# Transposes in front of the attention layer: from TensorE to transposing transfers, with the last products with V in another PSUM bank

## The chip, the cores and the metric

One Trainium2 chip, one core. The time is device microseconds for one execution, the median of the runs shown.

## What is computed

A two-layer decoder trunk on 256 tokens of width 1024, all in float32. The first layer mixes tokens with a gated recurrence, the second with attention whose logits carry a forget-gate bias; every layer has a SwiGLU half-step before and behind the mixer, and every part is wrapped in RMS norms. The part around the change, cut from the reference:

```python
f = swiglu(rms_norm(h, ffn1_pre_g), w_gate, w_up, w_down)
h = h + 0.5 * rms_norm(f, ffn1_post_g)
hn = rms_norm(h, mix_pre_g)
q = (hn @ w_q) * HEAD_DIM ** -0.5
logits = q @ k.T + c[q_rows] - c[k_rows]        # causal, 16 heads of 64
o = softmax(logits) @ v
h = h + rms_norm(o @ w_o, mix_post_g)
```

## The kernel before, in words

**Tiles.** The 256 tokens are two halves, t = 0 and t = 1, of 128 rows each; h0 and h1 hold them, 128 x 1024. TensorE is fed in a split form: a float32 operand is cut into a high and a low part (whi and wlo for weights, xhi and xlo for the stream), and a product is three matmuls, high by high, high by low, low by high. Weights come in pieces of 512 KB into five "raw" buffers (SP's queue issues the loads); ScalarE makes whi (L173) and VectorE wlo (L177), which also frees the raw buffer. Items with a load and a split are prepared ahead; a "slot" (t, i) is the work of item i for half t.

**From h to x.** A product needs x = h scaled by a gain, transposed: eight "k tiles" of 128 x 128. `enter` runs when a sub-layer's sums pf are done: sums of squares on ScalarE, the factor rstd on GpSimd, `t1 = pf * gain` and `h = t1 * rstd + h` on VectorE (L298, L311). Some ticks later `inputs` transposes h. There are two ways:

- On TensorE: `to_tp` (L226), four transposes per 512 columns into a PSUM bank; then VectorE multiplies by the gain (L234), ScalarE writes xhi (L235), VectorE writes xlo (L240).
- By a transposing transfer, for 512 columns: `planes` (L212, GpSimd) sorts the upper and lower 16 bits of each number into two planes, `swap` (L216) issues a DMA that transposes 16-bit elements, `join` (L220, GpSimd) puts the numbers together again; then the gain on VectorE and xhi on ScalarE (`turned_to_x`, L258 and L259), and xlo (L240).

Before the change the end of the half-step in front of attention uses TensorE for all eight k tiles of both halves.

**Queues.** TensorE's order is written out by hand: the stage around attention is the string ATT_ORDER, in which a digit is a slot of that half, l, n, t and v are logits, normalisation, transposes of the probabilities and products with V, each followed by the half. It begins `0 0 0 0 0 0 0 l0 0 1 n0 l0 1 1 t0 n0 1 l0 v0 1 t0 n0 l0 1`: eight slots of q for half 0 and then those of half 1, with the first half's softmax between them. `defer(n, fn)` calls fn n + 1 slots later. On VectorE, ScalarE, GpSimd and SP a scheduler decides the order at build time, and at run time each engine works through its queue strictly in that order.

**Attention.** `heads_T` scales the queries (L1044) and transposes them, on TensorE for half 0 (L1057), by a transfer for half 1. `logits` writes into two "gt" banks (L1194); VectorE adds the bias and takes the extreme (L1203), corrects it (L1207, L1208); ScalarE takes exponentials (L1210); VectorE normalises (L1216, L1217). `turn` transposes the result (L1223) and `values` multiplies with V into one of four "mm" banks, "po" (L1237). The bias of half 1 is a table of 2 MB in DRAM, fetched by GpSimd's queue at the start of the stage (`att_rows`, L1038).

**PSUM.** "mm" has four banks (sums of products), "gt" two (logits, transposes of h), "tr" two.

Of the kernel before, what the change touches and what calls it, by code (L numbers as in the profile page):

```python
# [17 lines left out]
P = 128  # L18
# [25 lines left out]
def trunk_kernel(ctx: ExitStack, tc: tile.TileContext, A: dict, out: bass.AP):  # L44
    nc = tc.nc
# [5 lines left out]
    hpool = ctx.enter_context(tc.tile_pool(name="h", bufs=1))  # L51
# [29 lines left out]
    def defer(n, fn):  # L81
        pend.append([n, fn])
# [23 lines left out]
    h = [hpool.tile([P, D], F32, tag=f"h{t}", name=f"h{t}") for t in range(2)]  # L106
# [23 lines left out]
    gT = cpool.tile([P, 56], F32, name="gT")  # L130
# [79 lines left out]
    def planes(dst, src):  # L210

        nc.gpsimd.tensor_copy(dst.rearrange("p (h f) -> p h f", h=2), src.bitcast(U16).rearrange("p (f h) -> p h f", h=2))  # L212

    def swap(turned, halves):

        tc.keep_in_program_order(nc.sync.dma_start(turned.rearrange("p (a b) -> p a b", b=P), halves, transpose=True))  # L216

    def join(dst, turned):

        nc.gpsimd.tensor_copy(dst, turned.rearrange("p (h f) -> p h f", h=2))  # L220
# [17 lines left out]
    def x_lower(xg, dest, n):  # L238
        gi, xh, xl = dest
        nc.vector.tensor_tensor(xl[:, 4 * n:4 * n + 4, :], xg, xh[:, 4 * n:4 * n + 4, :].bitcast(F32), ALU.subtract)  # L240
# [5 lines left out]
            for n, v in enumerate(xg):  # L246
                x_lower(v, dest, n)

    def turned_to_x(v, dests, more):

        with tc.high_priority():
            xs = []
            for i, (gi, xh, xl) in enumerate(dests):
                xg = v if i == len(dests) - 1 else more()
                g = gT[:, gi + 4:gi + 8].unsqueeze(2).to_broadcast([P, 4, P])
                xs.append(xg.rearrange("p (a b) -> p a b", a=4))
                tc.keep_in_program_order(
                    nc.vector.tensor_tensor(xs[i], v.rearrange("p (a b) -> p a b", a=4), g, ALU.mult))  # L258
                tc.keep_in_program_order(nc.scalar.activation(xh[:, 4:, :], xs[i], AF.Copy))  # L259
            for xg, dest in zip(xs, dests):  # L260
                x_lower(xg, dest, 1)

    def to_x_tiles(tps, dest):

# [15 lines left out]
    def stat(t):  # L280
        ss = new_ss()
        square_sum(h[t], ss[:, 0:1])
        rs[t] = rstd_of(ss, 1)

    def enter(t, dests, pf, gb, half, last=False, normed=False, wait=3, spare=None):
# [3 lines left out]
        t1 = []  # L289
# [26 lines left out]
        if last:  # L316
            return

        by_transfer = (spare or t == 1) and not (half and (len(dests) == 1 or t == 0)) and not normed
        if by_transfer:  # L320
            a = spare() if t == 0 else hpool.tile([P, 512], F32, tag="t1", name=nm("hp"), bufs=2)
            with tc.high_priority():
# [2 lines left out]
        def inputs():  # L325
            tps = [to_tp(h[t], n) for n in range(1 if by_transfer else 2)]
            for dest in dests:
                to_x(tps, dest)
            stat(t)
            if by_transfer:  # L330
                b = spare() if t == 0 else spool.tile([P, 512], F32, tag="junk", name=nm("ht"), bufs=1)
                with tc.high_priority():
                    swap(b.bitcast(U16), a.bitcast(U16))
                defer(0, lambda: join(a.bitcast(U16).rearrange("p (f h) -> p h f", h=2), b.bitcast(U16)))
                defer(1 + 2 * t, lambda: turned_to_x(a, dests, spare))

        def norm():
            with tc.high_priority():
# [22 lines left out]
        if normed:  # L361
            norm()
            settled[0] = True
        else:
            defer(wait, inputs)

    def gain_bcast(src):
        gb = hpool.tile([P, D], F32, tag="gb", name=nm("gb"), bufs=1)
# [239 lines left out]
    pools = {}  # L608
# [426 lines left out]
    def att_rows():  # L1035

        tc.keep_in_program_order(nc.scalar.activation(warm, mhalf, AF.Exp))
        tc.keep_in_program_order(nc.gpsimd.dma_start(att["bias1"], kv["bias1"]))  # L1038

    def heads_T(ps, t, n, scale, dst):  # L1040

# [130 lines left out]
    def attention(t):  # L1172
# [54 lines left out]
        def values(hg):  # L1227

            hds = range(hg * per, (hg + 1) * per)
            if hds[0] % 8 == 0:  # L1230
                box["po"] = mmbank()
            po, pT = box["po"].rearrange("p (a b) -> p a b", a=4), box["pT", hg]
            for j in range(0, per, 2):
                for k in range(nk):
                    for s in range(2):
                        hd = hds[j + s]
                        nc.tensor.matmul(po[s * HD:(s + 1) * HD, hd % 8 // 2, :], kv["v"][k][:, hd * HD:(hd + 1) * HD],  # L1237
                                         pT[:, (j + s) * nk + k, :], start=k == 0, stop=k == nk - 1)
# [266 lines left out]
```

## Time and profile before

| | us |
|---|---|
| median of 3 runs | 964.48 (964.27 to 964.72) |
| the profiled execution | 965.18 |
| its span in the trace | 963.5 |
| TensorE busy | 954.8 (99%) |
| VectorE, ScalarE, GpSimd busy | 646.0, 527.5, 236.5 |
| TensorE's granted clock | 0.999 |

The stage of the change lies between 700 and 770 us of the span: the half-step's last products end at 709, the queries' products run from 709 to 740, the softmax from 721 on, and w_o's products from 741 to 779. "Busy" of TensorE is modelled from the matmuls' sizes; waits are better seen in the distance between starts.

### The profile page before, as it was taken

The numbers are of one execution on the slowest core, as the hardware profiler recorded it, in microseconds if no ns is written. First come the engines' busy times: TensorE is split into PE (matmuls) and PEld (weight loads), VectorE is DVE, ScalarE is ACT, GpSimd is POOL, SyncE is SP. The second block draws the span as 40 slices with busy tenths as digits, with TensorE's granted clock in tenths as the row PEclk, the third lists the DMA queues.
The fourth block names the chain that finished last, engine by engine and source line by source line (L and its number), as shares of the span: only waits on it lengthen the run. The fifth ranks groups of instructions, "written<-read, shape, count | busy, mean of one in ns | idle before, by whom it ended". The sixth has DMA issues, their size and how long they took to land.

```text
span 963.5 us, 12847 instructions
## 1 busy us (share of the span) xinstructions
PE 954.8 (99%) x4559; PEld 789.6 (82%) x4559; DVE 646.0 (67%) x845; ACT 527.5 (55%) x750; POOL 236.5 (25%) x229
## 2 busy tenths in 40 slices
PE   9999999999999999999999999999999999999997
PEld 6888888898878888888898888888887788888885
DVE  6758774578997756664686566665488876666642
ACT  7446454568986555444565445444366865444431
POOL 2812230130003323230023623224022133232200
PEclk9999999999999999999999999999999999999999
DMA  8788996485338687676559979879763478777731
GB/s 283 227 229 252 250 291 196 143 222 166 128 110 244 203 238 215 201 245 193 138 158 313 249 223 262 223 190 289 227 255 102 121 210 260 208 225 234 217 110 44
DMA packets 153158, 199.84 MB, mean 207 GB/s; under 512 B 71390, under 2 KB 90182, under 8 KB 152966
## 3 DMA queue, kind: packets, MB, share of 16 engines
q1 hardware_dynamic: 150406, 192.11, 67.4%
q0 software_dynamic: 2080, 6.38, 2.3%
q8 instruction: 36, 0.59, 0.2%
q10 hardware_dynamic: 608, 0.53, 0.2%
q14 instruction: 28, 0.23, 0.1%
HBM read 182.19 MB, written 3.16 MB: 192 GB/s over the span
## 4 chain that ended last, share of the span: by engine, by line
PE 95%; DVE 2%; ACT 1%; issue 1%; POOL 0%; DMA 0%; POOLq 0%; DVEq 0%; ACTq 0%
PE mm L454 16%; PE mm L455 16%; PE mm L458 16%; PE mm L183 13%; PE mm L185 13%; PE mm L184 13%; PE gt L824 2%; PE mm L1340 1%; PE mm L190 1%; PE mm L191 1%; PE mm L192 1%; ACT pe L1210 1%; PE gt L226 1%; PE tr L127 0%; DVE wlo L177 0%
## 5 line engine op out<-in xcount | busy, mean ns | idle before, releaser
L177 DVE TENSOR_TENSOR wlo<-raw,whi 128x1024 fp32r<-128x1024 f32 (+5 forms) x329 | 423.0, 1293 | 213.9 <-ACT whi L173 212.4
L173 ACT ACTIVATE whi<-raw 128x1024 fp32r<-128x1024 f32 (+5 forms) x329 | 341.6, 1045 | 295.8 <-PE mm L458 107.2
L454 PE MATMUL mm<-whi,xhi 128*128 128x512 f32 x656 | 256.7, 391 | 0.0
L455 PE MATMUL mm<-wlo,xhi 128*128 128x512 f32 x656 | 255.5, 389 | 0.0
L458 PE MATMUL mm<-whi,xlo 128*128 128x512 f32 x656 | 202.2, 389 | 0.0
L454 PEld LDWEIGHTS mm<-whi,xhi 128*128 128x128 f32 x656 | 123.2, 188 | 25.9 <-issue 0.7
L458 PEld LDWEIGHTS mm<-whi,xlo 128*128 128x128 f32 x656 | 123.1, 188 | 26.0 <-DVE xlo L240 0.2
L455 PEld LDWEIGHTS mm<-wlo,xhi 128*128 128x128 f32 x656 | 123.2, 188 | 25.3 <-DVE wlo L177 0.3
L183 PE MATMUL mm<-whi,hhi 128*128 128x512 f32 x352 | 137.2, 390 | 0.0
L185 PE MATMUL mm<-whi,hlo 128*128 128x512 f32 x352 | 137.0, 389 | 0.0
L184 PE MATMUL mm<-wlo,hhi 128*128 128x512 f32 x352 | 137.0, 389 | 0.0
L569 POOL COPY pl<-prod 128x1024 uint16<-128x1024 uint16 (+1 forms) x48 | 67.7, 1410 | 168.9 <-DMA prod<-pl 168.9
L556 POOL COPY pl<-prod 128x1024 uint16<-128x1024 uint16 (+1 forms) x48 | 70.1, 1460 | 141.8 <-DVE prod L553 74.4
L185 PEld LDWEIGHTS mm<-whi,hlo 128*128 128x128 f32 x352 | 66.1, 188 | 13.7
L183 PEld LDWEIGHTS mm<-whi,hhi 128*128 128x128 f32 x352 | 66.1, 188 | 13.7
L184 PEld LDWEIGHTS mm<-wlo,hhi 128*128 128x128 f32 x352 | 66.1, 188 | 13.6
L198 POOL TENSOR_SCALAR nv<-ss 128x1 f32<-128x1 f32 x22 | 11.4, 517 | 252.8 <-ACT junk L205 252.8
L553 DVE SCALAR_TENSOR_TENSOR prod<-mm,rstd,sil 128x512 f32<-128x512 f32 (+1 forms) x48 | 33.7, 703 | 29.1 <-PE mm L458 24.8
L544 ACT ACTIVATE sil<-mm,rstd 128x512 f32<-128x512 f32 (+1 forms) x48 | 31.1, 650 | 32.4 <-PE mm L458 24.8
L575 DVE TENSOR_TENSOR hlo<-pl,hhi 128x512 fp32r<-128x512 f32 (+1 forms) x48 | 41.2, 858 | 3.6 <-ACT hhi L574 3.6
L183 PE MATMUL mm<-whi,xhi 128*128 128x512 f32 (+1 forms) x112 | 42.8, 382 | 0.0
L185 PE MATMUL mm<-whi,xlo 128*128 128x512 f32 (+1 forms) x112 | 42.5, 379 | 0.0
(235 smaller groups left out, 1067.8 us busy)
## 6 DMA issues: line engine op xcount, KB each, us to landing
raw<-in_ffn_w_down_dram SPq DMA_DIRECT2D x88, 512.0 KB
raw<-in_ffn_w_up_dram SPq DMA_DIRECT2D x80, 512.0 KB
raw<-in_ffn_w_gate_dram SPq DMA_DIRECT2D x78, 512.0 KB
raw<-in_rg_w_in_dram SPq DMA_DIRECT2D x10, 504.0 KB
raw<-in_rg_w_out_dram SPq DMA_DIRECT2D x10, 504.0 KB
raw<-in_ffn_w_gate_dram SPq DMA_DIRECT2D x19, 256.0 KB
raw<-in_ffn_w_up_dram SPq DMA_DIRECT2D x16, 256.0 KB
raw<-in_rg_w_in_dram SPq DMA_DIRECT2D x8, 512.0 KB
```

The costliest lines, as they stand in the source:

```text
L173: up = nc.scalar.activation(hi[:parts, c:c + m], rawv[:, c:c + m], AF.Copy)
L177: nc.vector.tensor_tensor(lo[:parts, c:c + m], rawv[:, c:c + m], hi[:parts, c:c + m].bitcast(F32), ALU.subtract)
L183: nc.tensor.matmul(ps, xh, wh, start=first, stop=False)
L184: nc.tensor.matmul(ps, xh, wl, start=False, stop=False)
L185: nc.tensor.matmul(ps, xl, wh, start=False, stop=last)
L454: nc.tensor.matmul(ps, get_x(t, k)[0], u.hi[:, c], start=k == 0, stop=False)
L455: nc.tensor.matmul(ps, get_x(t, k)[0], u.lo[:, c], start=False, stop=False)
L458: nc.tensor.matmul(ps, get_x(t, k)[1], u.hi[:, c], start=False, stop=k == nk - 1)
L553: nc.vector.scalar_tensor_tensor(pr[:, :nn], ps, rs[t][:, 0:1], s, ALU.mult, ALU.mult)
L556: nc.gpsimd.tensor_copy(halves.rearrange("p (h f) -> p h f", h=2), pr[:, :nn].bitcast(U16).rearrange("p (f h) -> p h f", h=2))
L569: nc.gpsimd.tensor_copy(halves.rearrange("p (f h) -> p h f", h=2), turned.rearrange("p (h a) b -> p h (a b)", h=2))
L575: keep(nc.vector.tensor_tensor(lv, x, hv.bitcast(F32), ALU.subtract))
```

## The change

At the end of the half-step in front of attention, half 0 now takes only its k tiles 0 to 3 through TensorE and 4 to 7 through one transposing transfer. Half 1 takes all eight through two transfers (`whole_inputs`), with planes made in `enter` itself. The fetch of the bias table is deferred by seven slots more. The products with V of the second eight heads of half 1 are summed in a "gt" bank in place of an "mm" bank.

```diff
-    def turned_to_x(v, dests, more):
+    def turned_to_x(v, dests, more, n=1):
...
-        by_transfer = (spare or t == 1) and not (half and (len(dests) == 1 or t == 0)) and not normed
+        by_transfer = (spare or t == 1) and not (half and len(dests) == 1 + (t == 0)) and not normed
+        whole = half and len(dests) == 1 and t == 1 and not normed
+        if whole:
+            with tc.high_priority():
+                hp = [hpool.tile([P, 512], F32, tag="t1", name=nm("hp"), bufs=2) for _ in range(2)]
+                for n in range(2):
+                    planes(hp[n].bitcast(U16), h[t][:, n * 512:(n + 1) * 512])
...
+        def whole_inputs():
+            ht = [pools["a"].tile([P, 512], F32, tag="pT", name=nm("ht"), bufs=4).bitcast(U16) for _ in range(2)]
+            with tc.high_priority():
+                for n in range(2):
+                    swap(ht[n], hp[n].bitcast(U16))
+            stat(t)
+            with tc.high_priority():
+                for n in range(2):
+                    join(hp[n].bitcast(U16).rearrange("p (f h) -> p h f", h=2), ht[n])
+            for n in range(2):
+                defer(3, lambda n=n: turned_to_x(hp[n], dests, None, n))
...
-            defer(wait, inputs)
+            defer(wait, whole_inputs if whole else inputs)
...
-        tc.keep_in_program_order(nc.gpsimd.dma_start(att["bias1"], kv["bias1"]))
+        defer(7, lambda: tc.keep_in_program_order(nc.gpsimd.dma_start(att["bias1"], kv["bias1"])))
...
-                box["po"] = mmbank()
+                box["po"] = mmbank() if t == 0 or hds[0] == 0 else gtbank()
```

`turned_to_x` with n = 0 writes k tiles 0 to 3, with n = 1 tiles 4 to 7. Line numbers behind `turned_to_x` rise by 18 in the changed kernel at most (L1203 becomes L1221).

Where this moves instructions, the built programs show. First VectorE, from the end of the half-step for half 1 to the first reductions of logits; before (h_75 is h1, xg the product of gain and turned h, htok the scaled queries, gt the logits, ISA the reduction):

```order
L177 TENSOR_TENSOR wlo_6338<-raw_6335,whi_6337 128x1024
L234 TENSOR_TENSOR xg_6383<-gt_6373,gT 128x512
L234 TENSOR_TENSOR xg_6386<-gt_6378,gT 128x512
L1044 TENSOR_SCALAR htok_6404<-mm_6354,rstd_6270 128x512
L240 TENSOR_TENSOR xlo<-xg_6383,xhi 128x4x128
L240 TENSOR_TENSOR xlo<-xg_6386,xhi 128x4x128
L1203 ISA pe_6443,mx_6442<-gt_6431,bias_2952 128x128
```

and the same place in the changed kernel (hp is h in planes and then turned):

```order
L177 TENSOR_TENSOR wlo_6341<-raw_6338,whi_6340 128x1024
L1062 TENSOR_SCALAR htok_6394<-mm_6356,rstd_6263 128x512
L258 TENSOR_TENSOR hp_6334<-hp_6334,gT 128x512
L240 TENSOR_TENSOR xlo<-hp_6334,xhi 128x4x128
L258 TENSOR_TENSOR hp_6335<-hp_6335,gT 128x512
L1221 ISA pe_6439,mx_6438<-gt_6427,bias_2952 128x128
L1221 ISA mx_6438 128x1
L240 TENSOR_TENSOR xlo<-hp_6335,xhi 128x4x128
L1221 ISA pe_6439,mx_6438<-gt_6428,bias_2952 128x128
```

Both multiplications by the gain, and with them the two joins, now stand ahead of the first reduction of the first half's logits, and the last low part behind the first reduction. Next GpSimd in the changed kernel, from the write of h1 on (before, the table's fetch, `L1038 DMA`, stood ahead of the first of these nv rows, and no hp row was there):

```order
L212 COPY hp_6334<-h_75 128x1024
L212 COPY hp_6335<-h_75 128x1024
L198 TENSOR_SCALAR nv_6382<-ss_6379 128x1
L200 TENSOR_TENSOR rstd_6384<-nv_6382,mhalf 128x1
L220 COPY hp_6334<-ht_6375 128x2x512
L220 COPY hp_6335<-ht_6376 128x2x512
L1056 DMA bias_6350<-bias1d 128x4096
L212 COPY pl_6535<-htok_6533 128x1024
```

Two planes, two joins and the fetch now stand in one row ahead of the second half's queries (pl and htok). And SP's queue in the changed kernel, from the last loads of w_q on:

```order
L161 DMA raw_6295<-in_attn_w_q_dram 128x2x512
L216 DMA_TRANSPOSE hp_6265<-hp_6217 128x8x128
L161 DMA raw_6301<-in_attn_w_q_dram 128x2x512
L164 DMA raw_6338<-in_attn_w_o_dram 128x1024
L164 DMA raw_6478<-in_attn_w_o_dram 128x1024
L164 DMA raw_6500<-in_attn_w_o_dram 128x1024
L164 DMA raw_6512<-in_attn_w_o_dram 128x1024
L387 DMA gb_6498<-in_mix_post_g_dram 128x1024
L216 DMA_TRANSPOSE ht_6375<-hp_6334 128x8x128
L216 DMA_TRANSPOSE ht_6376<-hp_6335 128x8x128
```

The three transposing transfers are new there: the first half's ahead of the last load of w_q, the second half's behind the gain row gb and ahead of w_o's fifth piece; the other rows keep their order. On VectorE the first half's multiplication stands between the splits of the sixth and seventh w_q pieces, and its low part between the two t1 rows of half 1. TensorE's order loses the three blocks of four transposes and is otherwise unchanged.

More of the change, by code (lines that the diff above doesn't have):

```diff
@@ L254, in turned_to_x @@
                 xg = v if i == len(dests) - 1 else more()
-                g = gT[:, gi + 4:gi + 8].unsqueeze(2).to_broadcast([P, 4, P])
+                g = gT[:, gi + 4 * n:gi + 4 * n + 4].unsqueeze(2).to_broadcast([P, 4, P])
                 xs.append(xg.rearrange("p (a b) -> p a b", a=4))
@@ L258, in turned_to_x @@
                     nc.vector.tensor_tensor(xs[i], v.rearrange("p (a b) -> p a b", a=4), g, ALU.mult))
-                tc.keep_in_program_order(nc.scalar.activation(xh[:, 4:, :], xs[i], AF.Copy))
+                tc.keep_in_program_order(nc.scalar.activation(xh[:, 4 * n:4 * n + 4, :], xs[i], AF.Copy))
             for xg, dest in zip(xs, dests):
-                x_lower(xg, dest, 1)
+                x_lower(xg, dest, n)
     def to_x_tiles(tps, dest):
```

## Prediction

> **What bounds the kernel now.** I read first the busy shares of the page and the chain that ended last, then TensorE's own waits, and then one stage, 700 to 770 us, row by row on each engine.
>
> ```profile
> PE 954.8 (99%) x4559; PEld 789.6 (82%) x4559; DVE 646.0 (67%) x845; ACT 527.5 (55%) x750; POOL 236.5 (25%) x229
> PE 95%; DVE 2%; ACT 1%; issue 1%; POOL 0%; DMA 0%; POOLq 0%; DVEq 0%; ACTq 0%
> PE gt L1194 <- POOL qT L220: 0.2, 1, 0.2
> ```
>
> TensorE is busy 99% and is 95% of the chain. TensorE's own list of waits has next to nothing in this stage; the one that matters is the last row. So an instruction taken off TensorE is time won, and a wait added on TensorE is time lost, since nothing behind has slack to win it back. The chain of waits inside this window leaves TensorE and comes back to it there:
>
> ```profile
> 722.54 0.47 PE mm L458 x2
> 723.03 0.75 DVE htok L1044
> 724.19 2.12 ACT pe L1210 x11
> ...
> 728.55 0.91 DVE wlo L177
> 729.70 0.76 DVE htok L1044
> 730.57 1.91 POOL pl L212
> 732.50 3.07 DMA htok<-pl
> 735.62 1.69 POOL qT L220
> 737.35 1.14 PE gt L1194 x8
> ```
>
> From the first half's softmax (exponentials on ScalarE from 724 on) through the second half's queries to the logits at 737.35 no link is idle. Whatever delays the softmax beyond its present place delays the logits by as much.
>
> **The change part by part: TensorE's instructions that go.** The timeline of TensorE, start and length:
>
> ```profile
> 702.69 0.39 PE L185 MATMUL mm<-whi,hlo 128*128 128x512 f32 x1
> 702.92 1.04 PE L226 MATMUL gt<-ident,h 128*128 128x128 f32 x8
> ...
> 704.02 0.39 PE L184 MATMUL mm<-wlo,hhi 128*128 128x512 f32 x1
> ...
> 771.06 0.60 PE L226 MATMUL gt<-ident,h 128*128 128x128 f32 x4
> ...
> 771.73 0.39 PE L184 MATMUL mm<-wlo,oh 128*128 128x512 f32 x1
> ```
>
> A matmul follows the next after 0.23 us (702.69 to 702.92). A block of eight costs 704.02 - 702.92 - 0.23 = 0.87 us, a block of four 771.73 - 771.06 - 0.23 = 0.44 us. The first half goes from eight to four, -0.43; the second from eight to none, -0.87. Sum **-1.30 us**.
>
> **The bank.** At the second half's first product with w_o:
>
> ```profile
> 763.60 0.40 PE L185 MATMUL mm<-whi,ol 128*128 128x512 f32 x1
> 764.08 0.50 PE L183 MATMUL mm<-whi,oh 128*128 128x512 f32 x1
> 764.41 0.39 PE L184 MATMUL mm<-wlo,oh 128*128 128x512 f32 x1
> ```
>
> Two steps take 0.81 where two free ones take 0.46: the second accumulator waits for a bank. With one tile more outside the four "mm" banks this wait has no cause, **-0.35 us**; at worst it stays, 0. The product moved into the logits' bank must now wait until VectorE has read the last logits there. It is the third product with V behind those logits, with two slots of w_o between, so I put it at 0; if VectorE falls behind TensorE there, the wait shows at that product.
>
> **What is added.** Each transfer is a copy on GpSimd (planes), a transposing transfer on SP's queue, a copy back on GpSimd (join), a multiplication on VectorE, and the two parts on ScalarE and VectorE. Rows for the same work elsewhere, and for the write of h0:
>
> ```profile
> 742.11 1.24 SPq L216 DMA_TRANSPOSE htok<-pl  x1
> ...
> 741.04 1.04 POOL L212 COPY pl<-htok 128x1024 uint16<-128x1024 uint16 x1 [3.74 <-DVE mx L1208]
> 745.27 1.37 POOL L220 COPY qT<-htok 128x1024 uint16<-128x1024 uint16 x1 [3.19 <-DMA htok<-pl]
> ...
> 766.42 1.90 POOL L212 COPY qT<-h 128x1024 uint16<-128x1024 uint16 x1 [1.58 <-DVE h L311]
> ...
> 700.89 1.42 DVE L311 SCALAR_TENSOR_TENSOR h<-t,rstd,h 128x512 f32<-128x512 f32 x2 [0.38 <-POOL rstd L200]
> ```
>
> A transfer is 3.1 us from issue to the copy it releases (742.11 to 745.27). A planes copy is 1.04 to 1.9 us; right behind the write of h, where VectorE goes on with weights, it is 1.90, and that case is ours. Joins run 1.37 to 1.7; I take 1.5.
>
> First half: h0 is written by 702.3 on VectorE (last row). Planes to 704.2, landed 707.3, join to 708.8, multiplication to 709.5, ScalarE's part to 710.3, VectorE's low part to about 711.9. TensorE, 0.43 earlier, wants the first at 711.55 (the slot at 711.98 today) and the second 0.9 later, at 712.45. Hidden, with 0.5 us left. It has a price all the same, for VectorE's order is fixed. Today:
>
> ```profile
> 708.03 2.35 DVE L177 TENSOR_TENSOR wlo<-raw,whi 128x1024 fp32r<-128x1024 f32 x2
> 710.30 1.28 DVE L298 TENSOR_TENSOR t<-mm,gb 128x512 f32<-128x512 f32 x2
> 711.51 1.41 DVE L311 SCALAR_TENSOR_TENSOR h<-t,rstd,h 128x512 f32<-128x512 f32 x2
> ```
>
> Between the two weight parts now stands the multiplication, which waits for the join until 708.8, and between the two t rows the low part. The write of h1 starts at about 712.5 and not at 711.51: 1.0 late, although TensorE ends earlier. SP's transfer stands ahead of the last load of w_q, which leaves some 2 us later for it; its use near 720 is far off, so that is free.
>
> Second half: the first half of h1 is there at 713.2. Planes to 715.1 and 717.0, landed 718.2 and 720.1, joins to 719.7 and 721.6, second multiplication about 721.7 to **722.3**. TensorE wants this x at 721.5 for tiles 0 to 3 (ready about 721.1) and at 724.6 for 4 to 7 (ready 723): hidden again. But VectorE's fixed order has the logits of the first half behind that multiplication. Today they start when TensorE delivers them:
>
> ```profile
> 721.44 0.29 DVE L1203 CUSTOM_DVE_ANT_0 pe<-gt,bias 128x128 f32<-128x128 f32 x1 [3.19 <-PE gt L1194]
> 723.70 0.15 DVE L1208 TENSOR_TENSOR mx<-mx,cq 128x4 f32<-128x4 f32 x1
> 725.78 0.69 DVE L1217 TENSOR_TENSOR pe<-pe,sm 128x512 f32<-128x512 f32 x1
> 727.40 0.60 PE L1223 MATMUL tr<-ident,pe 128*128 128x128 f32 x4
> ```
>
> TensorE would deliver at 720.1, and the 3.19 us of idle time in that row is the whole cover; the chain needs until 722.3. Behind the first reduction the last low part waits for ScalarE until 723.0 and ends at 723.6; three reductions (0.63), the queries' scaling (0.7) and the maximum (0.3) end at 725.3, where L1208 ends today at 723.8. So the softmax comes **1.5 us later than today**, where TensorE is 1.3 us earlier. The transposes at 727.40 have 0.9 us of slack today (pe is ready at 726.47): they wait until 728.0. The chain quoted above then carries the full 1.5 us to the logits at 737.35, which wait today already. The gain of 1.30 is thus consumed and 1.5 us added: TensorE waits some 2.8 us in all in two or three places (the transposes at 727.40 or the turned queries just ahead of them, and the logits at 737.35).
>
> The table bias1 is now fetched behind the joins:
>
> ```profile
> 711.49 0.63 POOL L1038 DMA_DIRECT2D bias<-bias1d  x1
> bias<-bias1d POOLq DMA_DIRECT2D x1, 2048.0 KB, 11.8
> 738.51 0.42 DVE L1203 CUSTOM_DVE_ANT_0 pe<-gt,bias 128x256 f32<-128x256 f32 x1 [0.41 <-PE gt L1194]
> ```
>
> Issued at 722 with 11.8 us it lands at 734, ahead of its use at 738.5 or later: 0. It leaves the queues free for the transposing transfers, which is in the 3.1.
>
> **Sum**: the stage ends at +1.5, the bank gives back 0.35, so **+1.15 us**. On the profiled execution (965.18, span 963.5) that is 966.33; on the median shown, 964.48, which lies 0.7 lower, it is **965.6**.
>
> Bounds. Everything hidden: -1.30 - 0.35 = -1.65. Copies as short as recorded (1.04 and 1.37): h1 0.9 earlier, planes done 2.6 earlier in all, and the multiplication, behind the low part of tiles 0 to 3, at 720.3: 2.0 less, net -0.85. On the other side a pair of transfers seen behind weight loads:
>
> ```profile
> 535.78 1.24 SPq L216 DMA_TRANSPOSE ktok<-pl  x1
> 537.76 1.43 SPq L216 DMA_TRANSPOSE ktok<-pl  x1
> ...
> 539.91 2.17 POOL L1072 COPY kT<-ktok 128x1024 uint16<-128x1024 uint16 x1 [2.18 <-DMA ktok<-pl]
> 542.52 2.29 POOL L1072 COPY kT<-ktok 128x1024 uint16<-128x1024 uint16 x1 [0.43 <-DMA ktok<-pl]
> ```
>
> 4.1 and 4.8 us to the copies, which themselves took 2.2: the same here adds 1.0 to 1.7 us to the +1.15, up to +2.9. I take 3.1, since the ring is nearer to that of 742.11: ahead of our transfers stand one load of w_o and the gain row, 2 us and more earlier.
>
> [...] The trace has the one at 742.11 moving at some 210 GB/s:
>
> ```profile
> GB/s 0 0 0 0 0 0 0 0 0 0 0 0 10 133 218 218 215 228 205 218 202 212 205 184 213 134 28 0 0 0 0 0 0 0 0 0 0 0 0 0
> ```
>
> **Rivals.** (1) The cover is long enough: copies find VectorE idle, the second multiplication ends by about 719.5 to 720.3, TensorE hardly waits, and the time is 962.8 to 963.6. For it: the 3.19 us of idle time on VectorE, and copies of 1.04. Against: it needs 2 us or more from a chain of seven links, and the copies right behind h in the rows are the long ones. (2) Slower: the two transfers of the second half come late, behind loads in SP's ring or because the first half's transfer moved h1. Place: the second join. Price: 1 us for each us, from the +1.15; it passes 0.2% (1.93 us, about what a measurement of this kernel can tell from no change) when the join ends 0.8 us later than 721.6. At the precedent's lengths: 966.6 to 967.4. If the first half's transfer takes 4.8 us too, TensorE waits at 712 as well and it is 969. (3) bias1 takes over 16 us, and the reductions at 738.5 wait: each us one us, 966 to 968; against it, w_o is loaded by then and little else wants the queues.
>
> **How the numbers follow.** My case (net -0.8 to +1.9) 0.62; rival 1, 0.11; rival 2, 0.22; rival 3, 0.05. No reckoned case gains over 1.93 us; I leave 0.04 of rival 1 for what I can't see. Faster 0.04, same 0.62 + 0.07 = 0.69, slower 0.27. The range, 963.0 to 967.4, takes in the short copies and the pair's lengths, and leaves out the fully hidden case and the slowest.
>
> **What would show it.** In the changed kernel's timeline: TensorE's blocks at 702.9 (four) and 713 (none); the second multiplication of hp ending near 722.3 and VectorE's first reduction right behind it; TensorE waiting near 726 to 728 for pe and before the second half's first logits, now near 738.9; no wait at the second half's second w_o accumulator. I am wrong if the first reduction starts by 720.8 (then a gain), or if the joins start after 719 and 721 (then rival 2).

## The result and the profile after

The changed kernel takes 967.74 us (median of 7 runs, 967.50 to 968.34), the kernel before 964.56 in the runs beside it: ratio 1.0032, 95% interval 1.0023 to 1.0042. That is 3.2 us slower, where the prediction had 1.15 and 967.4 as its upper end. The profiled execution took 967.74, its span is 966.0.

The profiled executions of the kernels here stand up to 2.6 us apart before the stage of the change begins (the write of h0 starts between 700.02 and 702.65). So times of different runs are compared here from one event: the first write of h0 at the end of the half-step (L311), at 700.89 before and 700.20 after. Where I write "on before's clock", 0.69 has been added to a time of after.

TensorE's list of waits after, with what it waited for, sum, times and longest:

```profile
PE tr L1075 <- DVE htok L1062: 2.5, 2, 2.0
PE tr L1241 <- DVE pe L1235: 1.0, 1, 1.0
...
PE gt L1212 <- POOL qT L220: 0.7, 1, 0.7
PE mm L476 <- DVE xlo L240: 0.2, 1, 0.2
```

Before, this list had two rows of the stage, 0.2 us each. Now the turned queries (htok), the probabilities (pe), the second half's queries (qT) and the first half's low part stand there with 4.4 us in all. The second and the third are in places that the prediction named, as is the shorter of the two waits in the first row (0.5 us). The 2.0 us at the first half's queries are in neither. TensorE's rows there:

```profile
702.22 0.60 PE L226 MATMUL gt<-ident,h 128*128 128x128 f32 x4
...
719.09 0.66 PE L1075 MATMUL tr<-ident,htok 128*128 128x128 f32 x4 [1.96 <-DVE htok L1062]
...
766.70 0.40 PE L185 MATMUL mm<-whi,ol 128*128 128x512 f32 x1
766.93 0.40 PE L183 MATMUL mm<-whi,oh 128*128 128x512 f32 x1
```

The block at 702.22 has four transposes and there is none near 713: the work has gone as reckoned. The last two rows are the place where half 1's second sum with w_o begins: a free step of 0.23 us, so the wait for a bank has gone too. Between starts more is lost than in the list of waits. On before's clock the same instructions of TensorE come 0.44 us earlier behind the first block of transposes, 0.2 later behind the first half's low part (0.64 lost), 0.6 earlier behind the second block, then 1.45 later at the turned queries, 2.1 at their second group, 3.4 at the probabilities, 3.85 at the second half's logits and, behind the bank, 3.45. What is new is on VectorE:

```profile
701.53 3.19 DVE L177 TENSOR_TENSOR wlo<-raw,whi 128x1024 fp32r<-128x1024 f32 x2
...
706.98 2.31 DVE L177 TENSOR_TENSOR wlo<-raw,whi 128x1024 fp32r<-128x1024 f32 x1
709.22 0.68 DVE L258 TENSOR_TENSOR hp<-hp,gT 128x512 f32<-128x512 f32 x1
709.82 1.21 DVE L177 TENSOR_TENSOR wlo<-raw,whi 128x1024 fp32r<-128x1024 f32 x1
...
713.00 1.42 DVE L311 SCALAR_TENSOR_TENSOR h<-t,rstd,h 128x512 f32<-128x512 f32 x2 [0.17 <-POOL rstd L200]
714.33 4.04 DVE L177 TENSOR_TENSOR wlo<-raw,whi 128x1024 fp32r<-128x1024 f32 x2
718.29 0.74 DVE L1062 TENSOR_SCALAR htok<-mm,rstd 128x512 f32<-128x512 f32 x1
720.57 1.72 DVE L258 TENSOR_TENSOR hp<-hp,gT 128x512 f32<-128x512 f32 x1 [1.54 <-POOL hp L220]
722.99 0.69 DVE L240 TENSOR_TENSOR xlo<-hp,xhi 128x512 fp32r<-128x512 f32 x1 [0.70 <-ACT xhi L259]
723.60 0.69 DVE L258 TENSOR_TENSOR hp<-hp,gT 128x512 f32<-128x512 f32 x1
724.20 0.29 DVE L1221 CUSTOM_DVE_ANT_0 pe<-gt,bias 128x128 f32<-128x128 f32 x1
```

The kernel before has between h0 and h1 also one split by itself and a pair of low parts:

```profile
705.69 1.21 DVE L177 TENSOR_TENSOR wlo<-raw,whi 128x1024 fp32r<-128x1024 f32 x1
706.82 1.28 DVE L240 TENSOR_TENSOR xlo<-xg,xhi 128x512 fp32r<-128x512 f32 x2
```

Compare the splits (wlo). Before, a pair took 2.35 us and one by itself 1.21. Here the pair at 701.53 takes 3.19, the one at 706.98 2.31 and the pair at 714.33 4.04; the multiplication at 720.57 takes 1.72, where one of its kind at 723.60 takes 0.69. GpSimd's copies lie beside exactly these:

```profile
701.68 1.97 POOL L212 COPY hp<-h 128x1024 uint16<-128x1024 uint16 x1 [1.51 <-DVE h L311]
...
706.77 1.51 POOL L220 COPY hp<-hp 128x1024 uint16<-128x1024 uint16 x1 [1.31 <-DMA hp<-hp]
...
713.82 3.48 POOL L212 COPY hp<-h 128x1024 uint16<-128x1024 uint16 x2 [0.85 <-DVE h L311]
...
719.19 2.61 POOL L220 COPY hp<-ht 128x1024 uint16<-128x1024 uint16 x2
```

Planes at 701.68 to 703.65, a join at 706.77 to 708.28, two planes at 713.82 to 717.30, two joins at 719.19 to 721.80. The split at 709.82, with no copy beside it, takes 1.21 again. VectorE had no idle time between h0 and h1 before, so h1 is written at 713.00, 713.69 on before's clock, in place of 711.51. From there the chain of waits runs on:

```profile
715.34 3.79 DMA ht<-hp
...
719.19 1.35 POOL hp L220
...
720.57 1.73 DVE hp L258
...
722.32 0.64 ACT xhi L259
...
723.02 0.57 issue
723.60 0.70 DVE hp L258
```

The second half's first transfer, its join, the first multiplication, its high part, the low part (the "issue" at 723.02 is its time) and the second multiplication are now one chain without a gap. Behind it stands the first reduction, at 724.20, or 724.89 on before's clock, 3.45 us later than before. The second half's logits follow at 740.51, 741.20 on that clock, where they were at 737.35.

### The profile page after: what moved, and what is told of

Its sections match the earlier page's. It is cut to its first block, busy times and chain, and to the rows that moved or that the text cites. A ratio compares the mean times of both kernels' runs of the same rounds, so it can differ in the third digit from the quotient of the medians.

```text
span 966.0 us, 12834 instructions
## 1 busy us (share of the span) xinstructions
PE 953.7 (99%) x4547; PEld 787.7 (82%) x4547; DVE 650.7 (67%) x845; ACT 527.2 (55%) x750; POOL 249.8 (26%) x235
## 4 chain that ended last, share of the span: by engine, by line
PE 92%; DVE 2%; issue 2%; ACT 1%; DMA 1%; POOL 1%; POOLq 0%; DVEq 0%; ACTq 0%
PE mm L472 16%; PE mm L473 15%; PE mm L476 15%; PE mm L183 13%; PE mm L185 13%; PE mm L184 12%; PE gt L842 2%; PE mm L1358 1%; PE mm L190 1%; PE mm L191 1%; PE mm L192 1%; ACT pe L1228 1%; DVE pe L1221 0%; DVE wlo L177 0%; PE tr L127 0%
## 5 line engine op out<-in xcount | busy, mean ns | idle before, releaser
L587 POOL COPY pl<-prod 128x1024 uint16<-128x1024 uint16 (+1 forms) x48 | 72.1, 1502 | 169.4 <-DMA prod<-pl 169.4
L574 POOL COPY pl<-prod 128x1024 uint16<-128x1024 uint16 (+1 forms) x48 | 72.0, 1501 | 134.2 <-DVE prod L571 71.1
```

What stands on the lines that cost most here:

```text
L574: nc.gpsimd.tensor_copy(halves.rearrange("p (h f) -> p h f", h=2), pr[:, :nn].bitcast(U16).rearrange("p (f h) -> p h f", h=2))
L587: nc.gpsimd.tensor_copy(halves.rearrange("p (f h) -> p h f", h=2), turned.rearrange("p (h a) b -> p h (a b)", h=2))
```

## The experiments

Theories when they began. **1**: GpSimd's copies and VectorE's instructions with two operands in SBUF hold each other up; the length that VectorE gains by it is what the prediction missed. **2** (rival): the order of VectorE's queue alone, the first reductions behind the multiplications, costs the time, and the longer rows cost nothing. **3** (rival): the transfers' traffic or the table's fetch. All fourteen runs, each timed beside the kernel before on the same chip; the third column is the start of h1's write behind that of h0's in the profiled execution, the last the last write of h behind that of h0 less the same of before (257.92):

| kernel | median us | less before | h0 to h1 | stage's loss |
|---|---|---|---|---|
| before | 964.6 to 964.9 | | 10.62 | 0 |
| after | 967.74 | +3.18 | 12.80 | +3.45 |
| bank_only | 964.28 | -0.60 | 10.62 | -0.34 |
| half0_only | 966.40 | +1.52 | 12.88 | +1.57 |
| half1_only | 966.46 | +1.58 | 10.63 | +0.72 |
| half1_bank | 966.49 | +1.87 | 10.62 | +1.74 |
| copies_act | 965.57 | +0.69 | 10.95 | +0.57 |
| after_act0 | 966.48 | +1.86 | 10.95 | +1.23 |
| half0_act | 964.66 | +0.03 | 10.96 | +0.09 |
| idle_transfer | 965.97 | +1.34 | 12.56 | +1.22 |
| idle_swap | 964.88 | +0.25 | 10.63 | 0.00 |
| order_late | 968.95 | +4.32 | 10.95 | +3.90 |
| half1_upper | 972.90 | +8.28 | 10.61 | +8.08 |
| half1_upper_act | 973.45 | +8.83 | 10.62 | +8.46 |
| half1_upper_defer | 966.35 | +1.61 | 10.62 | +1.79 |
| no_defer | 973.06 | +8.32 | 12.88 | +8.30 |

### The parts of the change, one by one

**bank_only**: the kernel before with

```diff
-                box["po"] = mmbank()
+                box["po"] = mmbank() if t == 0 or hds[0] == 0 else gtbank()
```

> The kernel before with one line changed: the products with V of the second eight heads of half 1 are summed in a gt bank. All theories expect the one step of 0.35 us in front of those products to go and nothing else to move: 964.2 us, a difference of -0.35 us from the kernel before. If the bank were taken from logits that still use it, a wait on the bank would stand in TensorE's list and the time would be the same or longer.

964.28 us, ratio 0.9994 (0.9985 to 1.0003). In the trace the end comes 0.34 us earlier, on before's clock, and no wait on the bank appears: the prediction's 0.35.

**half0_only**: the kernel before with the first half's transfer.

```diff
-        by_transfer = (spare or t == 1) and not (half and (len(dests) == 1 or t == 0)) and not normed
+        by_transfer = (spare or t == 1) and not (half and len(dests) == 1 + (t == 0)) and not normed
```

> The kernel before with only the first half's k tiles 4 to 7 through a transposing transfer. The prediction's sum: -0.43 us for four transposes, +0.2 for the short wait on the low part, so -0.2 us. Theory 1 (GpSimd's plane and join copies and VectorE's subtractions of two SBUF operands hold each other up, and the length that VectorE gains is what the prediction missed): the splits beside the planes and the join stretch from 2.35 to about 3.2 us a pair and from 1.2 to about 2.3 for the one, h1 is written 1 us later, and since half 1's transposes on TensorE follow h1 closely, the time comes to +0.3 to +1.0 us. Theory 2 (only the order on VectorE costs): the rows of the splits may be longer but nothing waits, -0.2 us.

966.40 us, ratio 1.0015 (1.0006 to 1.0024): +1.5, where the prediction's -0.43, with the wait of 0.2 seen in after, gave -0.2. The profiled execution is 1.76 us late from its start on. Its rows on VectorE, and TensorE's wait:

```profile
703.98 3.19 DVE L177 TENSOR_TENSOR wlo<-raw,whi 128x1024 fp32r<-128x1024 f32 x2
...
709.43 2.31 DVE L177 TENSOR_TENSOR wlo<-raw,whi 128x1024 fp32r<-128x1024 f32 x1
...
715.53 1.41 DVE L311 SCALAR_TENSOR_TENSOR h<-t,rstd,h 128x512 f32<-128x512 f32 x2 [0.25 <-POOL rstd L200]
```

```profile
PE gt L226 <- DVE h L311: 0.9, 1, 0.9
```

The two stretched splits, 0.84 and 1.10 us longer, are nearly the whole of h1's delay of 2.26, and TensorE waits for h1 at the transposes of half 1. The time is 0.5 above what theory 1 expected for this half (+0.3 to +1.0); theory 2's -0.2 is out.

**half1_only**: the changed kernel without the two parts above (half 1's two transfers and the deferred fetch are left).

> The changed kernel without the first half's transfer and without the gt bank: half 1's two transfers and the deferred table. Theory 1: the pair of splits beside the two planes is 4.0 us in place of 2.35, the scaled queries of half 0 and so TensorE's transposes of them are late, though less than the 1.96 us of the changed kernel, because h1 comes 1 us earlier: a stall of about 1.0, and +2.0 to +3.0 us in all. Theory 2 (the multiplications standing ahead of the reductions on VectorE is the whole cost): no stall at the transposed queries of half 0, softmax 1.5 us later, +0.6 us (+1.5 less 0.87 for eight transposes). Theory 3 (transfers slower than forecast): the planes-to-landing distance is over 3.5 us.

966.46 us, ratio 1.0020 (1.0011 to 1.0029), +1.6: below theory 1's range and above theory 2's. The pair of splits is 4.04 as in the changed kernel, but h1 is in its old place and there is no stall at the turned queries; TensorE waits 0.9 for the probabilities and 0.6 for half 1's queries. Theory 1's stall was wrong here. The mark that the expectation gives for slow transfers is met: from the issue of the first transfer at 713.36 to its join at 717.07 are 3.7 us, where 3.1 were forecast. The profiled execution, 965.62, lies 0.8 below the median, so the next run looks at this half again, with the bank.

**half1_bank**: the changed kernel with the line of half0_only taken back.

> The changed kernel without the first half's transfer alone (half 1's two transfers, the deferred table and the gt bank stay). Theory 1, with its amount: GpSimd's two copies of the first half are what makes h1 2.2 us late, and a late h1 is what brings the stall of 1.96 us at the turned queries. Without them h1 is in its old place, the stall is gone although the pair of splits beside half 1's planes still takes 4.0 us, and what is left is the wait of the first reductions for the second multiplication and the queries behind it (TensorE waits 0.9 for the first probabilities and 0.6 for half 1's queries): the time of half 1's transfers alone, 966.5, less 0.35 to 0.6 for the bank, 965.9 to 966.1. If the losses of the two halves simply add up (theory 2), it is the changed kernel less 1.5: 966.2; TensorE's list of waits tells the two apart.

966.49 us, ratio 1.0015 (1.0006 to 1.0024); the profiled execution took the median's time. Its chain of waits:

```profile
713.19 4.36 DMA ht<-hp
...
717.60 1.36 POOL hp L220
...
718.99 1.71 DVE hp L258
...
721.99 0.70 DVE hp L258
```

The transfer takes 4.36 us here, the first multiplication 1.71, because it runs beside the second join; in half1_only's profiled execution it took 0.70. So the second multiplication ends at 722.69, 723.34 on before's clock, 1.0 later than forecast although h1 is 1.0 earlier than I had put it. TensorE waits 1.0 for the probabilities, 1.0 for the second group of scaled queries and 0.6 for half 1's queries. The stall of 1.96 at the first group is gone, as expected, but the second group, which waits 0.5 in after, waits 1.0 here, and the time lies above both forecasts (965.9 to 966.1, and 966.2). The losses of the two halves nearly add up: +1.52 and +1.87 (with the bank) against 3.18.

### Is it GpSimd's copies, or the order, or the traffic?

**idle_transfer**: the kernel before, plus this, whose result nobody reads:

```diff
+        idle = half and len(dests) == 1 and t == 0 and not normed
+        if idle:
+            a = spare()
+            with tc.high_priority():
+                planes(a.bitcast(U16), h[t][:, 512:])
...
+            if idle:
+                b = spare()
+                with tc.high_priority():
+                    swap(b.bitcast(U16), a.bitcast(U16))
+                defer(0, lambda: join(a.bitcast(U16).rearrange("p (f h) -> p h f", h=2), b.bitcast(U16)))
```

> The kernel before, plus the first half's planes, transposing transfer and join as in the change, whose result nobody reads (all eight k tiles still come by TensorE; TensorE, VectorE and ScalarE have the same instructions in the same order as before). Theory 1 (GpSimd's copies and VectorE's instructions with two SBUF operands hold each other up): the pair of splits at 702 takes 3.2 us in place of 2.35, the one beside the join 2.3 in place of 1.2, h1 is written 1.9 us later, TensorE waits for it at half 1's transposes, and the time is 1.5 to 2.0 us longer. Theory 2 (only the order of VectorE's queue costs): nothing that VectorE or TensorE does has moved, so the time is that of before within 0.2 us. Theory 3 (the transfer's traffic disturbs the others): longer, and so is the next kernel.

965.97 us, ratio 1.0014 (1.0005 to 1.0023). VectorE's rows, then GpSimd's:

```profile
701.95 3.20 DVE L177 TENSOR_TENSOR wlo<-raw,whi 128x1024 fp32r<-128x1024 f32 x2
...
707.40 2.39 DVE L240 TENSOR_TENSOR xlo<-xg,xhi 128x512 fp32r<-128x512 f32 x2
...
713.18 1.40 DVE L311 SCALAR_TENSOR_TENSOR h<-t,rstd,h 128x512 f32<-128x512 f32 x2
```

```profile
702.10 1.97 POOL L212 COPY hp<-h 128x1024 uint16<-128x1024 uint16 x1 [1.51 <-DVE h L311]
...
707.18 1.52 POOL L220 COPY hp<-hp 128x1024 uint16<-128x1024 uint16 x1 [1.30 <-DMA hp<-hp]
```

The pair of splits is 0.85 longer; beside the join stand now the two low parts, 2.39 in place of 1.28. Sum 1.96, and h1 is 1.94 late. Nothing was moved on VectorE or TensorE and nothing waits for the copies: theory 1 is shown for this half, at 1.3 us of time (a little under its range), and order alone can't be the cause of it.

The rows show which instructions are held up: one with two operands in SBUF that comes to its turn while a GpSimd copy runs grows by 0.8 to 1.1 us in the rows shown; one that had begun before the copy does not (the low part at 706.38 in after, ahead of the join at 706.77, keeps its 0.68), nor do two with an operand in a PSUM bank that come to their turn during a join (in before, L1244 at 736.05 and L234 at 772.11 keep their 0.69 and 0.68); and with the copies on ScalarE (copies_act, below) none grows.

**idle_swap**: as idle_transfer, with the transfer alone, straight from h0, and no copy on GpSimd.

> The kernel before, plus the transposing transfer of half of h0 alone, without GpSimd's two copies; nobody reads it. Theory 1 and theory 2: no change, within 0.2 us. Theory 3 (the traffic of the transfer): a part of what the kernel with copies loses, over 0.5 us.

964.88 us, ratio 1.0001 (0.9992 to 1.0010), and no delay in the stage. For this half the transfer's traffic is out.

**copies_act**: the changed kernel with its six copies on the other engine:

```diff
-        nc.gpsimd.tensor_copy(dst, turned.rearrange("p (h f) -> p h f", h=2))
+        i = turned.rearrange("p (h f) -> p h f", h=2)
+        if act:
+            nc.scalar.activation(dst, i, AF.Copy)
+        else:
+            nc.gpsimd.tensor_copy(dst, i)
```

(planes likewise; act is set for the half-step in front of attention).

> The changed kernel with its six new plane and join copies on ScalarE in place of GpSimd; VectorE's order is nearly the same, with both multiplications still ahead of the first reductions. Theory 1: VectorE's splits return to 1.2 us each and its multiplication to 0.7, htok of half 0 is in time, the stall of 1.96 us at the transposed queries goes, and with it at least 1.5 of the 3.2 us: 966.2 us or less, as low as 963.5 if ScalarE's copies are also short enough to let the joins come early. Theory 2 (order alone): the rows shorten but the first reduction still waits for the second multiplication, and the time stays within 0.5 us of the changed kernel, 967.3 to 968. A rival within theory 1: ScalarE, 55% busy, delays the high parts by the copies' length and gives the time back, then a wait on ScalarE stands in TensorE's list.

965.57 us, ratio 1.0005 (0.9996 to 1.0014): 2.5 us of the 3.2 are gone. VectorE's rows:

```profile
713.76 2.35 DVE L177 TENSOR_TENSOR wlo<-raw,whi 128x1024 fp32r<-128x1024 f32 x2
716.03 0.74 DVE L1070 TENSOR_SCALAR htok<-mm,rstd 128x512 f32<-128x512 f32 x1
...
721.85 0.69 DVE L266 TENSOR_TENSOR hp<-hp,gT 128x512 f32<-128x512 f32 x1 [0.57 <-ACT hp L226]
722.46 0.28 DVE L1229 CUSTOM_DVE_ANT_0 pe<-gt,bias 128x128 f32<-128x128 f32 x1
```

The splits are back at 2.35, the scaled queries are 2.9 us earlier than after on one clock, the stall is gone. But the first reduction still stands right behind the second multiplication, and 0.7 us remain with 1.65 us of TensorE's work saved. That remainder fits theory 2, smaller than the whole; the chain of copies and transfers is long here too (10.0 us from the end of the write of h1's first part, at 712.58, to the end of the second multiplication, at 722.54, where the forecast had 9.1, from 713.2 to 722.3), and no run parts the two.

**after_act0**: only the first half's two copies on ScalarE.

> The changed kernel with only the first half's plane and join copies on ScalarE; half 1's four copies stay on GpSimd. Theory 1: the splits ahead of h1 are short again, h1 is 0.4 to 1.2 us late in place of 2.2, the pair of splits beside half 1's planes is still 4.0 us, and the stall at the turned queries is under 1 us in place of 1.96: 966.0 to 966.6, 1.1 to 1.7 less than the changed kernel. Theory 2 (order alone): 967.7.

966.48 us, ratio 1.0015 (1.0006 to 1.0024), 1.3 less than the changed kernel, as theory 1 had it. h1's first part is 0.33 late; its second stands behind a low part, takes 1.52 beside a planes copy in place of 0.74, and ends 1.7 late. The pair of splits is 3.19, not 4.0, since only the second planes copy now lies beside it, and the stall at the turned queries is 0.4.

**half0_act**: before with the first half's transfer, its copies on ScalarE, and the bank.

> The kernel before with the first half's tiles 4 to 7 by transfer, its plane and join copies on ScalarE in place of GpSimd, and the last products with V in a gt bank. Theory 1: the splits are back at 2.35 and 1.2 us, h1 is at most 0.4 us later than before (in the changed kernel with the copies on ScalarE it was 0.33 later, and its last part 1.2), and the sum is -0.43 for the transposes, -0.35 for the bank, up to +0.3 for the waits on the low part and on h1: 964.3 us, -0.5 from before, and 1.6 less than the two parts with GpSimd's copies add up to (+1.5 and -0.6). Theory 2 (order alone): as with GpSimd's copies, 965.5 to 966.

964.66 us, ratio 1.0001 (0.9992 to 1.0009). That is 0.9 less than half0_only and bank_only add up to, so the copies cost something here too; but my -0.5 was wrong. The saved transposes are used up:

```profile
711.12 0.74 DVE L319 SCALAR_TENSOR_TENSOR h<-t,rstd,h 128x512 f32<-128x512 f32 x1
711.77 0.68 DVE L248 TENSOR_TENSOR xlo<-hp,xhi 128x512 fp32r<-128x512 f32 x1
712.38 0.74 DVE L319 SCALAR_TENSOR_TENSOR h<-t,rstd,h 128x512 f32<-128x512 f32 x1
```

```profile
711.32 0.50 PE L462 MATMUL mm<-whi,xhi 128*128 128x512 f32 x1 [0.34 <-ACT xhi L267]
713.08 1.03 PE L234 MATMUL gt<-ident,h 128*128 128x128 f32 x8
```

The low part stands between the two writes of h1, whose second is 0.9 late, and TensorE waits 0.34 for a high part. Its transposes of half 1, at 713.08, are at 713.81 on before's clock and not at 713.35.

**order_late**: copies_act with half 1's second block asked for one slot later.

```diff
-                defer(3, lambda n=n: turned_to_x(hp[n], dests, None, n))
+                defer(3 + n, lambda n=n: turned_to_x(hp[n], dests, None, n))
```

> The changed kernel with its copies on ScalarE, and half 1's second turned block asked for one slot later, which puts the second multiplication by the gain behind the first reductions of the logits on VectorE (it stands behind seven of the eight, and on ScalarE its high part behind the exponentials); two loads on SP's queue also move ahead of the second half's transfer. If what is left of the loss (0.7 us above before, with 1.65 us of TensorE's work gone) is the wait of the first reduction for the second multiplication, the first reduction starts at about 721 in place of 722.5 and the scaled queries and the softmax follow 1 us earlier; then half 1's first product waits for its second high part, which now follows the exponentials: a new stall of 1 to 3 us on TensorE at the first xhi of the second block, and the time is longer than with the copies on ScalarE alone (965.6): 966 to 968. If there were cover enough for the later block, 964.5.

968.95 us, ratio 1.0042 (1.0030 to 1.0055), 1 us above the expected range. The first reduction starts at 720.79, or 721.3 on before's clock, as expected, and TensorE then waits for the second block's high part, which has moved behind the exponentials:

```profile
728.63 0.79 PE L480 MATMUL mm<-whi,xhi 128*128 128x512 f32 x1 [3.43 <-ACT xhi L267]
```

Both orders lose: with these transfers the time between h1 and the slot that needs it did not hold both the transfer's chain and the reductions. (The later block also moved two loads ahead of the second half's transfer.)

### Is there a half-way version?

**half1_upper**: before with the bank, and of half 1 only tiles 4 to 7 by transfer:

```diff
-        by_transfer = (spare or t == 1) and not (half and (len(dests) == 1 or t == 0)) and not normed
+        by_transfer = (spare or t == 1) and not (half and t == 0) and not normed
```

> The kernel before with the gt bank, and of half 1 only k tiles 4 to 7 by a transposing transfer with GpSimd's copies; tiles 0 to 3 and all of half 0 stay on TensorE. The planes fall on the pair of splits behind h1, the join into VectorE's empty time ahead of the first reductions (3.19 us idle before). Theory 1: the pair of splits is 3.2 us in place of 2.35, but the scaled queries still come 1 us ahead of TensorE's need, so stretching costs nothing here: -0.43 for four transposes and -0.35 to -0.6 for the bank, 963.6 to 964.0. If any GpSimd copy beside VectorE costs time whatever the slack: 964.5 to 965.5. If the one multiplication and low part are still late for the first reductions or for half 1's first product: over 965, with the wait in TensorE's list.

972.90 us, ratio 1.0081 (1.0067 to 1.0094). It is over 965 with the wait in TensorE's list (7.1 us for the second group of scaled queries), as in the third case, but for a reason and by an amount that no case had. The chain of waits:

```profile
714.08 0.03 POOL bias L1038
714.11 12.95 DMA ht<-hp
```

The table's fetch of 2 MB goes out 0.1 us ahead of the transfer, and the transfer takes 12.95 us. **half1_upper_act**, the same with the copies on ScalarE:

> As the kernel with tiles 4 to 7 of half 1 by transfer, with the two copies on ScalarE. Theory 1: VectorE's splits keep 2.35 us, which nobody needs here, and ScalarE's copy stands ahead of its table load and the sums: the same time within 0.3 us, 963.6 to 964.2.

973.45 us, ratio 1.0089 (1.0074 to 1.0104): it met the same wait (the fetch went out at 710.76, the transfer at 714.36, and the join started at 724.52) and says nothing of the copies.

**half1_upper_defer**: half1_upper with the fetch deferred as in the change.

> As the kernel with tiles 4 to 7 of half 1 by transfer and GpSimd's copies, now with the table's fetch deferred as in the change, so that it no longer stands ahead of the transfer. If the table's 2 MB held that transfer up (it was issued at 714.1, right behind the fetch at 714.0, and landed at 727.2), it now lands 3 us after its issue, at about 717.5, the join ends at 719, the multiplication and the low part stand in VectorE's idle time, and theory 1 gives -0.43 for four transposes and -0.35 to -0.6 for the bank although the pair of splits is still 3.2 us: 963.6 to 964.0. If GpSimd's copies cost time whatever VectorE's slack: 964.5 to 965.5. If the first reductions wait for the one multiplication: 964.5 to 965.5 too, with the wait on the probabilities in TensorE's list.

966.35 us, ratio 1.0015 (1.0006 to 1.0024), from 964.95 to 968.64, the profiled execution at 967.24: 6.6 less than half1_upper, and still above all three forecasts. The pair of splits takes 3.19 and TensorE does not wait for the first scaled queries, so stretching where VectorE has slack cost nothing there. But the join came late:

```profile
714.88 1.24 SPq L216 DMA_TRANSPOSE ht<-hp  x1
```

```profile
720.42 1.33 POOL L220 COPY hp<-ht 128x1024 uint16<-128x1024 uint16 x1 [3.75 <-DMA ht<-hp]
```

5.5 us from the start of the issue to the join, and the first reduction at 723.78 behind it. A piece of w_o had been issued on the same queue at 714.02. At this length even one transfer is too long for the place; whether one of 3.1 us would fit, no run shows.

**no_defer**: the changed kernel with the fetch in its old place.

> The changed kernel with the table's fetch in its old place, ahead of half 1's transfers. If the fetch of 2 MB holds the transfers up as it did the one: the joins come 9 to 10 us later, VectorE's order puts the multiplications behind the first reductions in part, TensorE waits for the scaled queries or for half 1's first high parts by 5 us or more, and the time is 972 to 978. If it was something else in that kernel (the buffer that its transfer writes), the time is that of the changed kernel, 967.7.

973.06 us, ratio 1.0087 (1.0073 to 1.0101), as expected if the fetch holds the transfers up; the other case, the buffer that the transfer of half1_upper writes, is out. The second half's first transfer, issued at 715.58 ahead of the fetch (717.48), reaches its join in 3.7 us; the second, right behind the fetch, takes 10.0 us in the chain of waits:

```profile
717.56 10.01 DMA ht<-hp
```

So the deferral, which moves nothing of its own, is worth 5.1 to 5.3 us to this change (8.32 - 3.18, or 973.06 - 967.74). All three kernels with the fetch ahead of a transfer show it late; what they share inside the DMA engines was not measured.

bank_only is the fastest of all: 3.5 us ahead of the changed kernel. Ahead of the kernel before it is 0.6 in the medians and 0.34 in the trace, with an interval that just includes 1.

## Why the prediction was wrong, step by step

- **Transposes removed, -1.30**: right. Four at 702.22, none at 713.
- **Bank, -0.35**: right (0.34 in bank_only's trace).
- **Table's fetch, 0**: right as far as it went (in after it took 8.2 us from 721.71, in time for the second half's logits); without the deferral the change costs over 5 us more, and the step did not say so.
- **First half's transfer, "Hidden", h1 "1.0 late"**: this is the step that failed. The low part came 0.2 us behind TensorE, which cost 0.64 between starts. h1 came 2.2 us late, of which the stretched splits are 1.94. The 1.0 had been put down to the multiplication's wait for the join and to the low part; the multiplication at 709.22 did not wait at all, and both only take the place of the same work that left its old one. So the cause was wrong and not only the size. The prediction had quoted both lengths of a planes copy, 1.04 and 1.90, and charged the conflict to GpSimd alone; VectorE, which had no idle time from h0 to h1, paid about as much again. The half costs +1.5 by itself, where the forecast had a gain of 0.43 and a late h1, and idle_transfer shows 1.3 us of loss from the copies alone.
- **Second half, "second multiplication about 721.7 to 722.3"**: the mechanism was right (VectorE's fixed order puts the reductions behind it, and the wait goes down the chain to the logits), the term too small by 2.7 us: it ended at 724.3, or 725.0 on before's clock. From the chain of waits: h1 1.2 later than I had put it, the transfer 3.79 in place of 3.1 (+0.7), the first multiplication 1.73 in place of 0.7 beside the second join (+1.0), the copies together some 0.4 shorter; the 0.2 left are spread over the links. Two of the three are the copies beside VectorE.
- **"the softmax comes 1.5 us later"**: 4.2 by the first L1208 (L1226 after, ending at 727.32, on before's clock 728.0 against 723.8). The logits of half 1 are 3.85 late. The forecast's sum with 4.2 in place of 1.5 would have been 3.85, against 3.45 in the trace and 3.2 in the medians. With the copies on ScalarE the kernel takes +0.7 (copies_act), near the +1.15 that the prediction gave to the kernel with GpSimd's, though not link for link (h1's write starts at 711.84 where the forecast had 712.5, and the second multiplication ends at 722.54 where it had 722.3).
- **The stall at the turned queries, 2.0 us**: not forecast. The pair of splits at 714.33 delays the scaling by 1.7 us more than h1 does. It seems to add little of its own, though no run takes it away alone: it is not on the chain of waits (the logits behind it start on TensorE at 721.06, and VectorE, held by the second multiplication, comes to them at 724.20).
- **Rival 2** (the second half's transfers late, behind loads "or because the first half's transfer moved h1") is the case that came, by the prediction's own mark: the joins start at 719.9 and 721.2 on before's clock, after 719 and 721. I had given it 0.22 and 966.6 to 967.4, or 969 if the first half's transfer were slow too, which it was not (3.1 us from issue to join). Its chance was too low because h1's term was short, its price because no case held the stretched multiplication.
- **VectorE beside the copies**: the rows of after show it held up at four splits and one multiplication, those whose turn came while one of the six copies ran: 0.84 us more for the pair at 701.53 (one split of it beside a copy), 1.10 for the split at 706.98, 1.69 for the pair at 714.33, 1.03 for the multiplication at 720.57.

Settled: the copies' effect (idle_transfer, copies_act), that the halves' losses nearly add, the fetch. Not settled: how much of what copies_act leaves is VectorE's order and how much the transfers, and why half 1's transfer takes between 3.7 and 5.5 us where 3.1 was seen elsewhere; loads of w_o stand ahead of it in SP's queue, but no run took them away.

## What to carry to other kernels

Before work moves to GpSimd, look at what VectorE does at that moment: here a planes copy that takes 1.04 us by itself took 1.97 beside splits with two operands in SBUF, and the pair of splits grew by 0.84, so the copy's length counted about once for each engine. Work taken off the busiest engine is a gain only if the replacement chain, from the last writer to the instruction that stands behind it in some other engine's fixed order, fits into the idle time of that engine; add the chain link by link and look for the first engine that has no idle time on the way. And a run that adds the suspected cost with nobody reading its result tells contention from waiting in one step.

## What the runs showed of the hardware

- A VectorE subtraction of two 128x1024 SBUF operands took 1.21 us alone and 2.1 to 2.3 when its turn came while a GpSimd copy ran; a 128x512 multiplication 0.69 and 1.72; the update of half of h 0.74 and 1.52 (after_act0). GpSimd's planes copy took 1.04 where no such instruction was under way when it began (741.04 before) and 1.97 behind one; with the copies on ScalarE the pairs of splits kept their 2.35 (copies_act).
- A transposing transfer of 256 KB on SP's queue took 3.1 to 5.5 us from its issue to the copy behind it with weight loads about, and 10.0 to 13.0 when a fetch of 2 MB on GpSimd's queue had been issued 0.1 to 3.6 us before it.
